# A fixed TensorE order from the last latents to the attention heads of a hybrid decoder layer

## The chip, the cores and the metric

One core of a Trainium2 chip runs the whole kernel. The core has a matrix engine (TensorE, in the rows PE, with its weight loads as PEld), a vector engine (VectorE, DVE), a scalar engine (ScalarE, ACT), a general engine (GpSimd, POOL) and a queue engine (SyncE, SP), which here only issues transfers. Each engine works through a queue of its own in order, and semaphores hold an instruction back until its inputs are there. The metric is the device time of one execution in microseconds; the kernel before takes 1210.38 us (median of 3 runs, 1208.66 to 1212.13).

## The reference, cut to what matters

A decoder layer for 256 tokens and a model width of 2048, all float32. After a norm, one input projection feeds two groups of heads: a recurrent group (RWKV-7, 16 heads of 64) and a latent attention group (8 heads of 128 with a rotary part of 64). Their outputs are concatenated and multiplied by `w_out`; a gated feed-forward block follows.

```python
y = rwkv7_scan(r, decay, k, v, -kk, kk * a)      # state of 64x64 per head, token by token
y = ((y - mu) * lax.rsqrt(var + GN_EPS)).reshape(bsz, s, c) * gn_w + gn_b
bonus = jnp.sum(r * k * r_k, axis=-1, keepdims=True) * v
y_rwkv = (y + bonus.reshape(bsz, s, c)) * g
...
q = (rms_norm(c_q, q_norm_g) @ w_uq)             # c_q, c_kv: latents of width 512
kv = (rms_norm(c_kv, kv_norm_g) @ w_ukv)
sc = (q_nope @ k_nope + q_pe @ k_pe) * scale     # causal, softmax, times v
...
y = jnp.concatenate([y_rwkv, y_mla], axis=-1)
x = x + y @ w_out[l]
```

## The kernel before, in words

**Products.** Every float32 weight piece of 128x1024 is loaded by SyncE (`raw`, L127), rounded by ScalarE to a high part (`hi`, L133) and completed by VectorE with a low part (`lo`, L134). Three buffers of each exist. A product is then three passes, high times high, high times low, low times high (`prod_b`, `prod_c`, `prod_a`, L160 to L197). Their results lie in three PSUM buffers named `mm`; two other PSUM sets, `ch` (three) and `at` (two), hold the small products.

**Input projection.** It runs over 35 tiles of 128 columns: first the decay, gate and key tiles, then `r` (9 to 16), `v` (17 to 24), and last eight tiles of latents (27 to 34), four for the queries and four for keys and values. `latent` (L767) scales a tile (`cr`), adds up its squares, splits it into `cl`, and at the end makes the inverse root `rr` (a chain of tiny GpSimd operations, `rsqrt`) and spreads it over all partitions by two products (`bcast`, `rrB`).

**Recurrence.** The 256 tokens are cut into four chunks of 64. Inside a chunk the token-by-token rule becomes a triangular solve. VectorE inverts 32x32 triangles for all heads in 62 dependent steps (`Tq`, L592 and L594), and GpSimd's queue moves them through DRAM to other partitions: `dT` and `dU` out (L596, L603), `TT` and `T11` back (L609, L605). TensorE joins the halves of each triangle (`pR`, L638, then `pT`, L651). `chunk(c)` (L674) then goes over the two halves `hf` of the head pairs. For each it makes `px` (state and local part), VectorE scales it to `XB`, TensorE multiplies by the triangle (`pu`, in the other half of `px`), VectorE and ScalarE copy it to `UV`, TensorE makes the state's change `pS` and the output `py`, VectorE updates the state `ST`, and ScalarE copies `py` to `yt`. A chunk needs the state of the one before.

**Heads.** `up_b` makes a piece of queries or keys from the latents, a loop at L833 the values. `group_norm(w)` normalises half of the recurrent output on VectorE, multiplies it by a gate (`pgate`, TensorE), and transposes it (`pyT`). `scores(h)` makes the masked scores of a head and its softmax (VectorE maximum, ScalarE exponential, VectorE scaling); `attend(h)` transposes them (`ptp`), copies them by ScalarE (`pT`) and multiplies by the values (`po`). The output product `wout` runs over two halves of its 2048 rows, the recurrent heads first, and the last four heads are traced inside its first half.

**Order.** Apart from a block for SyncE at the start (L328), the order of every engine is written by a planner: it goes through the traced instructions in a simulated run, and whenever an engine is free there it takes the ready instruction that was traced first. So later work, latents or queries, slips between the steps of the recurrence. `manual_schedule(engines=...)` instead keeps the traced order for the engines named inside the block; `issue_after(ins)` queues what it encloses behind `ins`.

Of the kernel before, what the change touches and what calls it, by code (L numbers as in the profile page):

```python
# [17 lines left out]
P = 128  # L18
T = 256
# [35 lines left out]
def hybrid_layer(ctx: ExitStack, tc: tile.TileContext, a: dict, out: bass.AP):  # L55
# [576 lines left out]
    for qh in range(2):  # L632
        pr_ = ch("pR")
        for q in range(16):
            qq = qh * 16 + q
            for h in range(2):
                o0 = h * 64 + 32
                PE.matmul(pr_[o0:o0 + 32, q * 32:(q + 1) * 32], G1[qq // 8][qq % 8 // 4][64:96, h * 4 + qq % 4, 32:64],  # L638
                          T11[h][64:96, qq, :], start=True, stop=True, tile_position=(64, o0))
        for h in range(2):  # L640
            o0 = h * 64 + 32
            V.tensor_tensor(RT[o0:o0 + 32, qh * 16:(qh + 1) * 16, :],
                            pr_[o0:o0 + 32].rearrange("p (q s) -> p q s", q=16),
                            mtok[o0:o0 + 32, qh * 16:(qh + 1) * 16].unsqueeze(2).broadcast_to([32, 16, 32]), ALU.mult)
    for qh in range(2):
        pr_ = ch("pT")
        for h in range(2):
            r0, o0 = h * 64 + 32, h * 64
            for q in range(16):
                qq = qh * 16 + q  # L650
                PE.matmul(pr_[o0:o0 + 32, q * 32:(q + 1) * 32], RT[r0:r0 + 32, qq, :],  # L651
                          TT[r0:r0 + 32, qq, 32:64], start=True, stop=True, tile_position=(r0, o0))
        for h in range(2):
            o0 = h * 64
            V.tensor_copy(TT[o0:o0 + 32, qh * 16:(qh + 1) * 16, 32:64],
                          pr_[o0:o0 + 32].rearrange("p (q s) -> p q s", q=16))
# [17 lines left out]
    def chunk(c):  # L674
        w, r = c // 2, c % 2
        rs_ = HS[r]
        for hf in range(2):
            px = ch("px")
            py = ch("py")

            def pairs(dst, terms):
                for n, term in enumerate(terms):
                    for a_ in range(4):
                        p = hf * 4 + a_
                        for h in range(2):
                            lhsT, rhs = term(p, a_, h)
                            PE.matmul(dst[HS[h], a_ * 64:(a_ + 1) * 64], lhsT, rhs,  # L687
                                      start=n == 0 and a_ == 0, stop=True, skip_group_check=True)
# [4 lines left out]
            def local(s):  # L693
                return lambda p, a_, h: (G1[c][hf][:, h * 4 + a_, s * 64:s * 64 + 64], UV[c][:, p, HS[h]])

            pairs(px, ([state(0)] if c > 0 else []) + [local(0)])
            for h in range(2):
                V.tensor_tensor(XB[hf][HS[h], :, HS[h]], px[HS[h], 0:256].rearrange("p (a v) -> p a v", a=4),
                                mtok[HS[h], c * 8 + hf * 4:c * 8 + hf * 4 + 4].unsqueeze(2).broadcast_to([64, 4, 64]),
                                ALU.mult)  # L700
            pu = px[:, 256:512]
            pairs(pu, [lambda p, a_, h: (TT[:, c * 8 + p, :], XB[hf][:, a_, HS[h]])])
            for h in range(2):
                (S.copy if h else V.tensor_copy)(UV[c][64:128, hf * 4:hf * 4 + 4, HS[h]],
                                                 pu[HS[h]].rearrange("p (a v) -> p a v", a=4))
            if c < 3:
                pS = ch("pS")
                pairs(pS, [lambda p, a_, h: (BKt[c][:, p, HS[h]], UV[c][:, p, HS[h]])])
            pairs(py, ([state(1)] if c > 0 else []) + [local(1)])
            if c < 3:  # L710
                for h in range(2):
                    hs = HS[h]
                    sv = ST[hf][hs, :, hs]
                    pSv = pS[hs, 0:256].rearrange("p (a v) -> p a v", a=4)
                    pcb = PC[hs, hf * 4:hf * 4 + 4, c:c + 1].broadcast_to([64, 4, 64])
                    if c > 0:
                        V.tensor_tensor(sv, pSv, sv, ALU.add)
                        V.tensor_tensor(sv, sv, pcb, ALU.mult)
                    else:
                        V.tensor_tensor(sv, pSv, pcb, ALU.mult)  # L720
            for h in range(2):
                yv = yt[w][rs_, hf * 512:(hf + 1) * 512].rearrange("p (a h v) -> p a h v", a=4, h=2)
                ylast[c] = S.copy(yv[:, :, h, :], py[HS[h], 0:256].rearrange("p (a v) -> p a v", a=4)).ins

    def group_norm(w):
# [19 lines left out]
        V.tensor_tensor(y, y, sq, ALU.add)  # L745
        for j in range(2):
# [4 lines left out]
            V.tensor_tensor(y[:, cs], y[:, cs], pg, ALU.mult)  # L751
        for j in range(2):
# [8 lines left out]
    for c in range(4):  # L761
        chunk(c)


    cl, rrs, rrB = [], [], []

    def latent(x, gname, post):  # L767
        c_ = [s4(F32R, "cl").rearrange("p (k s t) -> p k s t", k=2, s=2) for _ in range(2)]
        ssum = t2("css")
        for j in range(4):  # L770
            acc = in_tile(27 + x * 4 + j)
            cr = t2("cr")
            V.tensor_tensor(cr, acc[:, :T], rsB, ALU.mult)
            if j == 0:
                S.activation(ssum, cr, AF.Square)
            else:
                sq = t2("csq")
                S.activation(sq, cr, AF.Square)
                V.tensor_tensor(ssum, ssum, sq, ALU.add)
            h_, l_ = (c_[j // 2][:, j % 2, q, :] for q in range(2))  # L780
            S.activation(h_, cr, AF.Copy, scale=vv(gname, j))
            V.scalar_tensor_tensor(l_, cr, vv(gname, j), h_.bitcast(F32), ALU.mult, ALU.subtract)
        pss = at("pss")
        for tb in range(2):
            PE.matmul(pss[:, tb * 2:tb * 2 + 2], ssum[:, tb * P:(tb + 1) * P], ones[:, 0:2], start=True, stop=True)
# [4 lines left out]
        rb = con([P, T], f"rrB{x}")  # L790
        bcast(rr, rb, at, t2)
        rrs.append(rr)
        rrB.append(rb)
        cl.append(c_)

    latent(0, "qg", SC)
    latent(1, "kvg", 1.0)
    flush(True)
    qr = s4(n="qr").rearrange("p (h t) -> p h t", h=4)
# [6 lines left out]

    def up_b(src, i, x, dsts):
        pcs = piece(src[i])
        for j in range(2):
# [3 lines left out]
            V.tensor_tensor(dsts[j], acc[:, :T], rrB[x], ALU.mult)  # L813

    for i in range(4, 6):
        up_b(a["wuq"], i, 0, [qr[:, (i - 4) * 2 + j, :] for j in range(2)])
    for j in range(4):
        nc.gpsimd.dma_start(qs[j * 32:(j + 1) * 32], qr[(j ^ 1) * 32:(j ^ 1) * 32 + 32])
    V.tensor_tensor(qr, qr, cosR.unsqueeze(1).broadcast_to([P, 4, T]), ALU.mult)
    V.tensor_tensor(qs, qs, sinR.unsqueeze(1).broadcast_to([P, 4, T]), ALU.mult)  # L820
    V.tensor_tensor(qr, qr, qs, ALU.add)
    g2a = s4(n="g2a")
    g2b = s4(n="g2b")
    gnwb = [s4(n=n) for n in ("gnw", "gnb")]
    with tc.issue_after(ylast[1]):
        for t, n in zip(gnwb, ("gnw", "gnb")):
            nc.scalar.dma_start(t, a[n].broadcast_to([P, 1024]))
        nc.scalar.dma_start(g2a, a["g2"][0:P])
        nc.scalar.dma_start(g2b[64:96], a["g2"][P:160])
# [3 lines left out]
    for cc in range(2):  # L833
        accs = [mm() for _ in range(2)]
        for i in range(2):
            prod_a(accs, piece(a["wuv"][cc, i]), lambda k: cl[1][k // 2][:, k % 2, 0, :],
                   lambda k: cl[1][k // 2][:, k % 2, 1, :],
                   i * 2, 2, i == 0, i == 1)
        for tb in range(2):
# [40 lines left out]
    for i in range(4):  # L880
        up_b(a["wuq"], i, 0, [qn[:, i * 2 + j, :] for j in range(2)])
        up_b(a["wuk"], i, 1, [kn[:, i * 2 + j, :] for j in range(2)])

    def heads(*hs):
        for h in hs:
            scores(h)
            if h > 0:
                attend(h - 1)

    group_norm(0)  # L890
    heads(0, 1)
    group_norm(1)
    heads(2, 3)
# [11 lines left out]
    for half in range(2):  # L905
        if half == 1:
            attend(7)
            zs = [hl4("z") for _ in range(4)]
        for c in range(4):
            accs = [mm() for _ in range(2)]  # L910
            for i in range(4):
                if half == 0 and i == 2:
                    load_x1(c)
                    heads(4 + c)
# [4 lines left out]
            if half == 1:  # L919
# [180 lines left out]
```

## Time and profile before

| | |
|---|---|
| median of 3 runs | 1210.38 us (1208.66 to 1212.13) |
| profiled execution | 1211.12 us, its span 1209.3 us |
| TensorE busy | 1166.8 us, 96% of the span, 7633 products |
| VectorE busy | 819.8 us, 68% |
| ScalarE busy | 583.2 us, 48% |
| GpSimd busy | 82.1 us, 7% |
| mean granted TensorE clock | 0.985 |
| DMA, mean over the span | 179 GB/s |

The span runs from the first to the last instruction. A row of the timeline names start, duration, engine, line, operation, output and inputs and a count; in square brackets stands how long the engine was idle before it and what ended that wait. A wait row has the waiting instruction on the left, its releaser on the right, then the sum, the number and the longest. The granted clock is a share of full speed, and the stretch that the change touches runs from about 221 to 475 us.

### The profile page before, as it was taken

To read this page: it belongs to the slowest core of one execution; us is meant where nothing else is said; L and a number is where in the kernel's file an instruction comes from. 1 tells how busy PE (TensorE), PEld (TensorE's weight loads), DVE (VectorE), ACT (ScalarE), POOL (GpSimd) and SP (SyncE) were. 2 spreads that over 40 slices of the span, in tenths; PEclk is the share of its full clock that TensorE was granted. 3 is DMA by queue.
4 is the path that set the end of the run, shared out by engine and by line. 5 is a ranking of instruction groups with operands and counts; after the bars stand their busy time and mean duration, and the time that the engine had idled before them with its cause. 6 is when DMAs were issued, how large, how long until landed. Compare 5 with 4: busy or idle time off the path is not lost.

```text
span 1209.3 us, 19618 instructions
## 1 busy us (share of the span) xinstructions
PE 1166.8 (96%) x7633; PEld 1029.2 (85%) x7633; DVE 819.8 (68%) x1304; ACT 583.2 (48%) x883; POOL 82.1 (7%) x248
## 2 busy tenths in 40 slices
PE   7899989988798999999999999999999999999996
PEld 7899989987686888888888888888888888888885
DVE  6797659766777556777777776444577777775563
ACT  6674335432334445655555554333455555554442
POOL 1500430301101001000000000000000000000000
PEclk9999999988899999999999999999999999999998
DMA  8555454734142555555555555556655555566672
GB/s 325 164 159 158 147 167 156 209 108 144 54 157 85 170 187 184 183 188 192 190 192 190 191 191 191 191 191 191 205 194 187 192 192 190 192 219 209 209 211 85
DMA packets 61486, 215.90 MB, mean 179 GB/s; under 512 B 7376, under 2 KB 8144, under 8 KB 61392
## 3 DMA queue, kind: packets, MB, share of 16 engines
q1 hardware_dynamic: 58544, 209.22, 52.8%
q0 software_dynamic: 2080, 3.38, 1.3%
q10 hardware_dynamic: 768, 2.05, 0.5%
q8 instruction: 60, 0.98, 0.3%
q14 instruction: 34, 0.28, 0.1%
HBM read 210.48 MB, written 3.41 MB: 177 GB/s over the span
## 4 chain that ended last, share of the span: by engine, by line
PE 87%; DVE 5%; POOL 2%; DMA 2%; ACT 2%; issue 1%; SPq 0%; ACTq 0%; DVEq 0%; POOLq 0%
PE mm L163 27%; PE mm L166 13%; PE mm L195 9%; PE mm L196 9%; PE mm L197 9%; PE mm L175 9%; PE mm L178 4%; PE pg L536 1%; DVE lo L134 1%; DMA T<-dU 1%; ACT hi L133 1%; DMA xraw<-in_xT 1%; PE py L687 1%; PE px L687 1%; POOL sinR L304 0%
## 5 line engine op out<-in xcount | busy, mean ns | idle before, releaser
L134 DVE TENSOR_TENSOR lo<-raw,hi 128x1024 fp32r<-128x1024 f32 x376 | 460.2, 1224 | 287.6 <-ACT hi L133 281.3
L133 ACT CAST hi<-raw 128x1024 fp32r<-128x1024 f32 x376 | 394.9, 1050 | 490.6 <-issue 223.6
L163 PE MATMUL mm<-z,hi 128*128 128x512 f32 x1408 | 351.3, 392 | 0.0
L163 PEld LDWEIGHTS mm<-z,hi 128*128 128x128 f32 x1408 | 251.9, 188 | 43.7
L166 PEld LDWEIGHTS mm<-z,lo 128*128 128x128 f32 x1408 | 188.3, 188 | 14.5
L166 PE MATMUL mm<-z,lo 128*128 128x256 f32 x1408 | 191.6, 278 | 0.0
L175 PE MATMUL mm<-x,hi 128*128 128x256 f32 x1056 | 147.8, 289 | 14.5 <-ACT hi L133 8.1
L175 PEld LDWEIGHTS mm<-x,hi 128*128 128x128 f32 x1056 | 135.4, 195 | 17.1 <-ACT hi L133 8.1
L196 PE MATMUL mm<-lo,hh 128*128 128x512 f32 x336 | 130.7, 389 | 0.0
L197 PE MATMUL mm<-hi,hl 128*128 128x512 f32 x336 | 130.7, 389 | 0.0
L195 PE MATMUL mm<-hi,hh 128*128 128x512 f32 x336 | 119.7, 389 | 0.0
L178 PE MATMUL mm<-x,lo 128*128 128x256 f32 x528 | 77.4, 286 | 0.0
L197 PEld LDWEIGHTS mm<-hi,hl 128*128 128x128 f32 x336 | 63.1, 188 | 13.2
L195 PEld LDWEIGHTS mm<-hi,hh 128*128 128x128 f32 x336 | 63.1, 188 | 13.0
L196 PEld LDWEIGHTS mm<-lo,hh 128*128 128x128 f32 x336 | 63.1, 188 | 13.0
L178 PEld LDWEIGHTS mm<-x,lo 128*128 128x128 f32 x528 | 69.6, 193 | 0.2
L196 PE MATMUL mm<-lo,yhi 128*128 128x512 f32 x128 | 51.5, 403 | 0.0
L197 PE MATMUL mm<-hi,ylo 128*128 128x512 f32 x128 | 50.5, 394 | 0.0
L195 PE MATMUL mm<-hi,yhi 128*128 128x512 f32 x128 | 49.7, 406 | 0.0
L974 POOL MEMSET gt<- 128x2 f32 x44 | 4.3, 99 | 575.9 <-DVE hl L986 559.0
L197 PEld LDWEIGHTS mm<-hi,ylo 128*128 128x128 f32 x128 | 24.2, 189 | 5.1
L196 PEld LDWEIGHTS mm<-lo,yhi 128*128 128x128 f32 x128 | 24.2, 189 | 5.0
(282 smaller groups left out, 1113.1 us busy)
## 6 DMA issues: line engine op xcount, KB each, us to landing
raw<-in_wgu SPq DMA_DIRECT2D x176, 512.0 KB, 3.3
raw<-in_wdn SPq DMA_DIRECT2D x88, 512.0 KB, 4.2
raw<-in_win SPq DMA_DIRECT2D x70, 512.0 KB, 3.6
raw<-in_wout SPq DMA_DIRECT2D x32, 512.0 KB, 3.6
raw<-in_wuq SPq DMA_DIRECT2D x6, 512.0 KB, 4.0
xraw<-in_xT SPq DMA_DIRECT2D x4, 512.0 KB, 6.3
xt<-in_x SPq DMA_DIRECT2D x4, 512.0 KB, 6.8
raw<-in_wuv SPq DMA_DIRECT2D x4, 512.0 KB, 3.8
```

What stands on the lines that cost most here:

```text
L133: S.copy(hi, raw)
L134: last_lo[0] = V.tensor_tensor(lo, raw, hi.bitcast(F32), ALU.subtract).ins
L163: PE.matmul(acc, hi[:, j * P:(j + 1) * P], act(kt0 + j), start=first and j == 0, stop=False, skip_group_check=True)
L166: PE.matmul(acc[:, :T], lo[:, j * P:(j + 1) * P], act(kt0 + j)[:, 0, :], start=False, stop=last and j == n - 1, skip_group_check=True)
L175: PE.matmul(acc, hi[:, j * P:(j + 1) * P], act(kt0 + j)[:, s, :], start=first and j == 0 and s == 0, stop=False, skip_group_check=True)
L178: PE.matmul(acc, lo[:, j * P:(j + 1) * P], act(kt0 + j)[:, 0, :], start=False, stop=last and j == n - 1, skip_group_check=True)
L195: PE.matmul(accs[tb], ah, wh, start=first and j == 0, stop=False)
L196: PE.matmul(accs[tb], ah, wl, start=False, stop=False)
L197: PE.matmul(accs[tb], al, wh, start=False, stop=last and j == n - 1)
L536: PE.matmul(pg[h][:, o:o + P], BK[pp][hs, gg, w * 2 + r, :, :], AR[pp][hs, gg, w * 2 + r, :, :], start=o == 0, stop=True, skip_group_check ...
L687: PE.matmul(dst[HS[h], a_ * 64:(a_ + 1) * 64], lhsT, rhs, start=n == 0 and a_ == 0, stop=True, skip_group_check=True)
L974: nc.gpsimd.memset(gt[:, 0:2], 0.0)
```

## The change

The last latents, the joining of the triangles, the recurrence, the group norms' products, the queries, keys and values and the heads 0 to 5 (with the scores of head 6) are put in one block in which TensorE's order is the traced one. Only the first three tiles of the query latent are traced ahead of it, and stay with the planner.

The loops over `pR` and `pT` become `solve_r` and `solve_t`, unchanged. Each chunk is cut into three steps, and each step runs over both halves: `chunk_a` makes `px`, and for chunks after the first the state's part of `py`; `chunk_b` makes `pu`; `chunk_c` makes `pS` and the local part of `py`. `px` now lies in the `at` buffers, `py` and `pS` in `ch`. Between the steps a generator hands out big products in units: half a latent tile, one piece of queries or keys, or half a piece of values, 24 in all. The group norm is cut into a VectorE part, a gate and an output part.

The query latent's inverse root is no longer spread and multiplied into the queries: ScalarE copies them as they are, and the root goes into the softmax, as the scale of the exponential and a product with the maximum. The halves of the output product change places: the attention rows come first, with the scores of head 7 and the last two `attend` inside its first column block.

```diff
+    def solve_r():
...
+    def solve_t():
...
-    def chunk(c):
+    def chunk_a(c):
         for hf in range(2):
-            px = ch("px")
-            py = ch("py")
+            px[hf] = at("px")
+            if c > 0:
+                py[hf] = ch("py")
+                pairs(py[hf], hf, [state(1)])
+            pairs(px[hf], hf, ([state(0)] if c > 0 else []) + [
+                lambda p, a_, h: (G1[c][hf][:, h * 4 + a_, 0:64], UV[c][:, p, HS[h]])])
...
+    def chunk_b(c):
+        for hf in range(2):
+            pu = px[hf][:, 256:512]
+            pairs(pu, hf, [lambda p, a_, h: (TT[:, c * 8 + p, :], XB[hf][:, a_, HS[h]])])
...
+    def chunk_c(c):
+        for hf in range(2):
             if c < 3:
                 pS = ch("pS")
+                pairs(pS, hf, [lambda p, a_, h: (BKt[c][:, p, HS[h]], UV[c][:, p, HS[h]])])
...
+        for hf in range(2):
+            if c == 0:
+                py[hf] = ch("py")
+            pairs(py[hf], hf, [...], c == 0)
...
+    def latent_tile(x, j, gname):
...
+        prod_c(acc, piece(a["win"][i, 0]), x_hl, 0, 8, True, False)
+        yield
+        prod_c(acc, piece(a["win"][i, 1]), x_hl, 8, 8, False, True)
...
-            V.tensor_tensor(dsts[j], acc[:, :T], rrB[x], ALU.mult)
+            if x == 0:
+                S.copy(dsts[j], acc[:, :T])
+            else:
+                V.tensor_tensor(dsts[j], acc[:, :T], rrB1, ALU.mult)
...
             V.tensor_reduce(mx[:, qb:qb + 1], psc[:, ks], AX.X, ALU.max, negate=True)
-            S.activation(pe_[:, ks], psc[:, ks], AF.Exp, bias=mx[:, qb:qb + 1], accum_out=sm[:, qb:qb + 1])
+        V.tensor_tensor(mx, mx, rrs[0], ALU.mult)
+        for qb in range(2):
+            ks = slice(qb * P, qb * P + (qb + 1) * P)
+            S.activation(pe_[:, ks], psc[:, ks], AF.Exp, bias=mx[:, qb:qb + 1], scale=rrs[0][:, qb:qb + 1],
+                         accum_out=sm[:, qb:qb + 1])
...
+    for j in range(3):
+        for _ in latent_tile(0, j, "qg"):
+            pass
...
+    def all_units():
+        yield from latent_tile(0, 3, "qg")
+        for j in range(4):
+            yield from latent_tile(1, j, "kvg")
+            if j == 0:
+                latent_rs(0, SC)
+        up_b(a["wuq"], 4, 0, [qr[:, j, :] for j in range(2)])
+        yield
+        latent_rs(1, 1.0)
+        up_b(a["wuq"], 5, 0, [qr[:, 2 + j, :] for j in range(2)])
+        rope_q()
+        yield
...
+        bcast(rrs[1], rrB1, mm, t2)
+        up_b(a["wuk"], 0, 1, [kn[:, j, :] for j in range(2)])
+        yield
+        yield from up_v(0)
...
+    with tc.manual_schedule(engines={mybir.EngineType.PE}):
+        solve_r()
+        unit(2)
+        solve_t()
+        chunk_a(0)
+        unit(2)
+        chunk_b(0)
+        unit()
+        chunk_c(0)
+        for c in range(1, 4):
+            unit()
+            chunk_a(c)
+            unit()
+            chunk_b(c)
+            unit()
+            chunk_c(c)
...
+        gn_vec(0)
+        gn_vec(1)
+        unit(2)
+        scores(0)
+        unit()
+        scores(1)
+        attend(0)
+        gn_gate(0)
+        unit()
+        gn_out(0)
+        attend(1)
+        scores(2)
+        unit()
+        scores(3)
+        attend(2)
+        unit()
+        attend(3)
+        unit(2)
+        gn_gate(1)
+        scores(4)
+        unit()
+        scores(5)
+        attend(4)
+        gn_out(1)
+        unit()
+        attend(5)
+        scores(6)
...
-    for half in range(2):
-        if half == 1:
-            attend(7)
+    for half in (1, 0):
+        if half == 0:
             zs = [hl4("z") for _ in range(4)]
...
-                if half == 0 and i == 2:
+                if half == 1 and i == 2:
                     load_x1(c)
-                    heads(4 + c)
+                if half == 1 and c == 0 and i in (1, 2, 3):
+                    (scores(7), attend(6)) if i == 1 else attend(7) if i == 3 else None
```

More of the change, by code (lines that the diff above doesn't have):

```diff
@@ L631, in hybrid_layer @@
     RT = sv("RT").rearrange("p (q s) -> p q s", q=32)
[L632 to L635, printed above, removed]
+    def solve_r():
+        for qh in range(2):
+            pr_ = ch("pR")
+            for q in range(16):
+                qq = qh * 16 + q
+                for h in range(2):
+                    o0 = h * 64 + 32
+                    PE.matmul(pr_[o0:o0 + 32, q * 32:(q + 1) * 32], G1[qq // 8][qq % 8 // 4][64:96, h * 4 + qq % 4, 32:64],
+                              T11[h][64:96, qq, :], start=True, stop=True, tile_position=(64, o0))
@@ L645, in hybrid_layer @@
[L645 to L656, printed above, removed]
+                V.tensor_tensor(RT[o0:o0 + 32, qh * 16:(qh + 1) * 16, :],
+                                pr_[o0:o0 + 32].rearrange("p (q s) -> p q s", q=16),
+                                mtok[o0:o0 + 32, qh * 16:(qh + 1) * 16].unsqueeze(2).broadcast_to([32, 16, 32]), ALU.mult)
@@ L670, in hybrid_layer, with pairs @@
     ylast = [None] * 4
-    def chunk(c):
-        w, r = c // 2, c % 2
-        rs_ = HS[r]
-        for hf in range(2):
-            px = ch("px")
-            py = ch("py")
[L681 to L688, printed above, removed]
+    def pairs(dst, hf, terms, first=True):
+        for n, term in enumerate(terms):
+            for a_ in range(4):
+                p = hf * 4 + a_
+                for h in range(2):
+                    lhsT, rhs = term(p, a_, h)
+                    PE.matmul(dst[HS[h], a_ * 64:(a_ + 1) * 64], lhsT, rhs,
+                              start=first and n == 0 and a_ == 0, stop=True, skip_group_check=True)
@@ new lines, in hybrid_layer, with unit @@
+    units = all_units()
+    def unit(n=1):
+        for _ in range(n):
+            next(units)
+    with tc.manual_schedule(engines={mybir.EngineType.PE}):
[14 more added lines that the diff above has]
+            chunk_c(c)
+        g2a = s4(n="g2a")
+        g2b = s4(n="g2b")
+        gnwb = [s4(n=n) for n in ("gnw", "gnb")]
+        with tc.issue_after(ylast[1]):
+            for t, n in zip(gnwb, ("gnw", "gnb")):
+                nc.scalar.dma_start(t, a[n].broadcast_to([P, 1024]))
+            nc.scalar.dma_start(g2a, a["g2"][0:P])
+            nc.scalar.dma_start(g2b[64:96], a["g2"][P:160])
+        gn_vec(0)
[25 more added lines that the diff above has]
+        scores(6)
+        assert next(units, None) is None
```

138 lines of the change are left out of this document (63 added, 75 removed).

## The prediction

> **What bounds the kernel now.** I read the page first (the engines' shares: TensorE is busy 96% of a span of 1209.3 us, nothing else over 68%), then the table of stretches, then the waits of TensorE inside the stretch that the change touches, from the last latents to the end of the output product. In the table of stretches the columns are length, busy time with count for PE, PEld, DVE, ACT, POOL, then the granted clock, DMA share and GB/s.
>
> ```profile
> PE 1166.8 (96%) x7633; PEld 1029.2 (85%) x7633; DVE 819.8 (68%) x1304; ACT 583.2 (48%) x883; POOL 82.1 (7%) x248
> ```
>
> ```profile
> 221.00:475.00 254.00, 235.71 (x2053) 202.55 (x2052) 167.97 (x268) 101.13 (x173) 26.50 (x69) 0.95 0.45 141
> 254.00:261.00 7.00, 7.00 (x62) 6.82 (x59) 3.74 (x6) 1.04 (x1) 0.00 (x0) 0.51 0.16 64
> 295.00:301.00 6.00, 5.05 (x89) 4.87 (x91) 3.54 (x8) 1.10 (x3) 0.00 (x0) 0.50 0.48 157
> 322.00:330.00 8.00, 6.92 (x68) 6.32 (x67) 5.09 (x9) 3.94 (x8) 0.00 (x0) 0.57 0.57 192
> 373.00:377.00 4.00, 3.13 (x13) 3.06 (x14) 2.67 (x6) 1.68 (x4) 0.00 (x0) 0.57 0.00 0
> ```
>
> The first row holds everything that can be won: 254.0 - 235.7 = 18.3 us in which TensorE does nothing. The other four rows are the places where it works at about half the clock; busy time times the missing share of the clock is 7.00 x 0.49 + 5.05 x 0.50 + 6.92 x 0.43 + 3.13 x 0.43 = 3.4 + 2.5 + 3.0 + 1.3 = 10.2 us. Together 28.5 us are lost in this stage, and a perfect order of TensorE could win no more.
>
> The waits of TensorE in the same stretch (us in all, times, longest) say where the 18.3 us lie:
>
> ```profile
> PE px L687 <- DVE XB L698: 5.5, 5, 2.7
> PE pyT L755 <- DVE yt L751: 4.1, 1, 4.1
> PE mm L178 <- DVE lo L134: 2.0, 1, 2.0
> PE pS L687 <- DVE UV L704: 2.0, 3, 0.8
> PE py L687 <- DVE ST L717: 1.9, 1, 1.9
> PE pR L638 <- DMA T<-dU: 1.4, 1, 1.4
> ```
>
> The recurrence (the px, pS and py rows) and the group norm (pyT) cost most; the wait for the solved triangles (pR, for T) costs only 1.4 us. Why only 1.4 is what this prediction turns on, so the timeline of TensorE around it comes next (start, duration, instruction, count):
>
> ```profile
> 221.45 2.04 PE L175 MATMUL mm<-x,hi 128*128 128x256 f32 x16
> ...
> 224.28 2.05 PE L175 MATMUL mm<-x,hi 128*128 128x256 f32 x16
> ...
> 241.69 0.63 PE L175 MATMUL mm<-x,hi 128*128 128x256 f32 x4
> 243.77 0.28 PE L638 MATMUL pR<-T,G 32*32 32x32 f32 x4 [1.45 <-DMA T<-dU]
> ...
> 246.41 2.21 PE L638 MATMUL pR<-T,G 32*32 32x32 f32 x124
> 248.54 0.71 PE L237 MATMUL rsb<-dg,ones 128*128 128x128 f32 x4
> ...
> 250.78 4.30 PE L651 MATMUL pT<-TT,RT 32*32 32x32 f32 x128
> ```
>
> Up to 241.69 TensorE multiplies latents (L175): half a latent tile every 224.28 - 221.45 = 2.83 us. They are the filler under which the triangles go through DRAM. Where the third latent tile ends follows from VectorE, which reads each finished tile once (L773), and the chain of T from VectorE's last step and GpSimd's queue:
>
> ```profile
> 221.65 0.42 DVE L773 TENSOR_TENSOR cr<-mm,rsB 128x256 f32<-128x256 f32 x1 [0.35 <-PE mm L178]
> ...
> 224.62 1.22 DVE L134 TENSOR_TENSOR lo<-raw,hi 128x1024 fp32r<-128x1024 f32 x1
> 225.76 0.21 DVE L594 TENSOR_TENSOR Tq<-Tq,tm 128x31 f32<-128x31 f32 x1
> ```
>
> ```profile
> 226.28 1.00 POOL L596 DMA_DIRECT2D dT<-Tq  x1 [36.62 <-DVE Tq L594]
> 227.44 1.00 POOL L603 DMA_DIRECT2D dU<-tp  x2 [0.17 <-issue]
> 232.14 3.16 POOL L609 DMA_DIRECT2D TT<-dT  x4 [3.69 <-DMA dT<-Tq]
> 235.29 0.79 POOL L605 DMA_DIRECT2D T<-dU  x1
> ...
> 236.39 0.81 POOL L605 DMA_DIRECT2D T<-dU  x1
> ```
>
> ```profile
> qs<-qr POOLq DMA_DIRECT2D x4, 128.0 KB, 3.6
> ...
> T<-dU POOLq DMA_DIRECT2D x2, 128.0 KB, 8.4
> ```
>
> The third finished latent tile is read at 221.65 (the earlier ones 5.66 us apart); the triangles are done at 225.97, go out, come back, and the second T lands at 236.39 + 8.4 = 244.8.
>
> **The change part by part.**
>
> *Wait for T.* The new order puts only the first three latent tiles ahead of the fixed block, and the block begins with the pR products. Everything that TensorE did from 221.45 to 241.69 now stands behind pR in its queue: the fourth tile of the first latent, the second latent, and through them all units, steps, heads. So TensorE arrives at 221.45 and stands. What VectorE does up to that point is the same program, so Tq ends hardly earlier: one split (the lo at 224.62) falls away, because three pieces are then already held and TensorE frees none; 1.2 us. T is then issued last at about 235.2. How long it takes to land is unknown, since hardly any weights are then loading beside it: between 3.6 us (qs, the same size, but not through DRAM) and 8.4 us (now). It lands between 238.8 and 243.6; I take the middle, 241.2. The wait is 20 us (17.4 to 22.2).
> The Trainium skill, in "DMA: Bandwidth & Descriptors", section Specifications, gives 512 bytes as the least run for full rate. T is stored to DRAM and reread in runs of 32 floats, 128 bytes, and by that rule the missing weights would help it little and the wait would be the 22 us of the upper end; the trace has the 8.4 us, but none without weights beside it.
>
> *What is removed.* At best the whole 28.5 us: all waits, T's 1.4 among them, and all half clock. Row by row: px waits for XB, pS for UV and py for ST get a unit of 2.83 us between the steps, which is longer than the longest of them (2.7). The 4.1 us for yt go because the gate of the second half now stands eight units later. The rrB broadcast of the first latent (L237) goes, at most 0.7 us; I take 0.5. Its 12 multiplications move from VectorE to a ScalarE copy and the softmax gets one tiny product more per head; I cost both at nothing: three mm buffers and a unit of 2.83 us cover the copy, and without that cover each of the 12 would cost its 0.42 us (the L773 row, same shape), 5 us in all, which the high end of the units below includes.
>
> *New half clock.* After 20 us of standing TensorE starts pR at half clock. The nearest rows are the 4.1 us wait (373 to 377: 1.3 us lost) and the run of small products (254 to 261: 3.4 us lost; there it had been busy with pT from 250.78 on and the clock still fell). I take 3.4 for the start, and half of another 3.4 for pT, which again runs 4.3 us of 32x32 products alone: 5 us (1.3 to 8).
> The Trainium skill's page "TensorE: Matmul & The Clock Gate", Part 1, has the clock halve after an idle window of some 3.4 us and return after as long a busy one; by that the start would cost 1.7 us. The 7 us at half clock from 254 agree with the drop but not with so quick a return.
>
> *New waits in the recurrence.* A step now belongs to both halves, and three `ch` buffers hold py, py and one pS. So the second pS must wait until VectorE has read the first.
>
> ```profile
> 281.04 0.87 DVE L717 TENSOR_TENSOR ST<-pS,ST 64x256 f32<-64x256 f32 x2
> ```
>
> That is 0.9 us plus some 0.3 of signals, or up to 1.2 more when a split or a step of the group norm (the lo row and the yt row below) is under way: 1.2 to 2.4 for chunks 1 and 2, less for chunk 0 (py waits there): 3 to 7.
>
> ```profile
> 371.78 1.22 DVE L745 TENSOR_TENSOR yt<-yt,gsq 128x1024 f32<-128x1024 f32 x1
> ```
>
> ```profile
> L133 ACT CAST hi<-raw 128x1024 fp32r<-128x1024 f32 x376 | 394.9, 1050 | 490.6 <-issue 223.6
> ```
>
> VectorE's own work per chunk (14 operations of about 0.42, as the two of the L717 row, and three splits of 1.22, near 11 us with a latent tile's) fills most of the 12 us of a chunk, so XB and ST slip past their 2.83 us now and then: 0 to 4. I take 6 us together (3 to 11).
>
> *New waits in the heads.* In `attend` the three transposes are followed at once by po, which needs ScalarE's copy. Now:
>
> ```profile
> 360.76 0.38 PE L872 MATMUL ptp<-cst,pexp 128*128 128x128 f32 x2
> ...
> 361.18 0.48 ACT L873 COPY pT<-ptp 128x384 f32<-128x384 f32 x1 [1.65 <-PE ptp L872]
> ...
> 361.84 0.59 PE L875 MATMUL po<-pT,vm 128*128 128x256 f32 x2
> ```
>
> From the transposes' end (361.14) to po it takes 0.7 us, filled at present with another head's scores. Six `attend` lie in the fixed block: 0.7 each, or 1.75 behind one of ScalarE's casts of 1.05 (the L133 row); 4.2 to 10.5, I take 6. The softmax has one unit and one score ahead of its transposes (about 4.3 us), and the two group norms, traced before the heads, put VectorE operations of 1.22 us ahead of their maxima and of the splits: 0 to 7, I take 3. The output product now begins with the attention half, whose last two heads are just being made: 0 to 3, I take 1. New waits: 6 + 6 + 3 + 1 = 16 (7 to 31; not all will be at their worst, so I carry 25).
>
> *Sum.* New losses 20 + 5 + 16 = 41 (25.7 to 55) against 28.5 + 0.5 removed: +12 us (-3 to +26). The profiled execution took 1211.1 us, its span and 1.8 us around it, and lies 0.7 above the median of the runs. 1211.1 + 12 = 1223.1, against the median 1222.4: I say 1222.
>
> **The rivals.**
>
> 1. *The steps are covered (faster).* Place: the gaps between the steps of each chunk and after each ptp. Each old wait was at most 2.7 us and each unit is 2.83, which speaks for it. If units cover all but the floor of the `attend` copies (4.2), T lands as fast as qs (17.4), and the clock recovers in 1.3, new losses are 22.9 against 29: -6, 1204 us. It decides from the point where all new waits after T stay under 29 - 20 - 5 = 4 us with my T; the six copies alone use 4.2, which speaks against it. Chance 0.14.
>
> 2. *It evens out.* The idle time is only moved: one long wait in place of many. With T at its fast end (17.4), 3 us of half clock and 8 of new waits, 28.4 against 29: 1210 us. For it: VectorE does the same work in the stage (168 of 254 us). Against it: the wait for T has no cover at all now. Chance 0.14.
>
> 3. *VectorE becomes the bound of the heads (slower still).* Both group norms (some eight operations of 1.22 us each, near 20 us) come up when the last chunk ends, ahead of splits and maxima; TensorE's fixed order can no longer slip other work in. With T at 22, half clock 7 and new waits 25 the sum is 54 - 29 = +25: 1235 us. Against it: in the stretch VectorE is busy only 168 of 254 us. Chance 0.14.
>
> 4. *The wait for T doesn't come.* The block's first products might still be passed by later latents, if the order did not bind TensorE. Then the recurrence alone is rearranged: 29 - 16 - 5 = 8 us won, 1202 us. Nothing in the trace speaks for it: the pR products now already make TensorE stand while L175 work is at hand. Chance 0.03; it goes with the faster cases.
>
> **How the numbers follow.** The forecast (slower, +4 to +20 us, 1214 to 1230) has 0.55. Anything within 0.3% (3.6 us) counts as no change here, as the runs before spread that far. Slower: 0.55 + 0.14 + a part of the second case that ends above +3.6 = 0.71. Faster: 0.14 + 0.03 less what stays within 3.6 us = 0.14. Same: 0.15. The range takes in the first rival's price at its low end and the third's at its high end: 1204 to 1235.
>
> **What would show it.** Right: the longest wait of TensorE is pR for T, 17 to 22 us, beginning near 221.5 with pR's start near 241; the px and ST waits of the recurrence fall under 1 us each; pS waits for ST in chunks 1 and 2 (1 to 2.5 us); po waits for pT six times, about 1 us each; the clock is near 0.5 for some us behind pR. Wrong: a wait for T under 12 us, or sums of waits behind T under 4 us, would turn the sign; a group norm row (yt or gva) at the head of TensorE's or VectorE's waits would mean the third rival.

## The result, and the profile after

The changed kernel takes 1241.66 us (median; 1235.73 to 1243.22) against 1209.52 us for the kernel before on the same chip: a ratio of 1.0246, 95% interval 1.0225 to 1.0267. It is slower, as forecast, but by some 32 us, not 12, and it lies above the range.

The page of the changed kernel, shares of the engines and the slices of the span (40 equal ones of 31 us):

```profile
PE 1173.2 (95%) x7629; PEld 1031.4 (83%) x7629; DVE 815.6 (66%) x1297; ACT 588.7 (47%) x895; POOL 82.8 (7%) x248
...
PE   7899989599759999999999999999999999999996
...
PEclk9999999689959999999999999999999999999998
```

The span grew from 1209.3 to 1240.8 us, by 31.5. TensorE is busy 6.4 us more for four products fewer, which fits the lower clock (17.1 us lost to it against 10.2, worked out below); the other 25 us are idle time. TensorE's share sags in slice 8 and in slices 11 and 12, its clock in slices 8 and 9 and in slice 12. The waits of TensorE in the changed kernel (us in all, times, longest) name them:

```profile
PE ptp L899 <- DVE pexp L891: 17.0, 1, 17.0
PE pR L640 <- DMA T<-dU: 15.1, 2, 14.6
...
PE po L902 <- ACT pT L900: 4.4, 5, 1.8
...
PE pS L685 <- DVE ST L728: 3.0, 2, 1.9
PE py L685 <- DVE UV L713: 1.8, 2, 1.2
PE py L685 <- DVE ST L731: 0.8, 1, 0.8
```

The first two waits make 17.0 + 15.1 = 32.1 us. The rows of before that were to go (px for XB 5.5, pyT for yt 4.1, mm for lo 2.0) are gone. The table of stretches of the changed kernel, same columns as before:

```profile
236.00:246.00 10.00, 9.37 (x160) 9.20 (x161) 3.36 (x5) 1.05 (x1) 0.00 (x0) 0.58 0.01 3
250.00:259.00 9.00, 9.00 (x127) 8.82 (x123) 4.88 (x10) 0.89 (x1) 0.00 (x0) 0.62 0.19 60
284.00:290.00 6.00, 4.95 (x64) 4.87 (x65) 4.13 (x11) 1.46 (x4) 0.00 (x0) 0.72 0.25 87
322.00:328.00 6.00, 5.95 (x30) 4.75 (x31) 5.95 (x8) 3.17 (x6) 1.72 (x2) 0.72 0.54 175
336.00:353.00 17.00, 0.13 (x1) 0.13 (x1) 13.46 (x21) 3.14 (x9) 5.10 (x14) 0.62 0.17 62
353.00:367.00 14.00, 13.43 (x30) 6.75 (x31) 5.05 (x9) 0.85 (x2) 0.00 (x0) 0.50 0.00 0
```

Busy time times the missing share of the clock gives 3.9 us behind the first long wait, 3.4 behind the transposed triangles, 1.4 and 1.7 in the recurrence, and 6.7 behind the second long wait: 17.1 us, where the kernel before lost 10.2.

What TensorE waits for from 336 to 353 is in VectorE's timeline of the changed kernel (start, duration, instruction):

```profile
328.62 1.22 DVE L744 TENSOR_REDUCE gmu<-yt 128x16 f32<-128x1024 f32 x1
...
333.29 1.23 DVE L752 TENSOR_TENSOR yt<-yt,ry 128x1024 f32<-128x1024 f32 x1 [2.20 <-POOL ry L228]
...
340.22 1.22 DVE L760 TENSOR_TENSOR yt<-yt,gsq 128x1024 f32<-128x1024 f32 x1
342.62 1.22 DVE L750 TENSOR_REDUCE gva<-gsq 128x16 f32<-128x1024 f32 x1 [1.18 <-ACT gsq L748]
343.88 2.45 DVE L757 TENSOR_TENSOR gsq<-UV,bon 64x1024 f32<-64x1024 f32 x2
346.34 0.62 DVE L882 TENSOR_REDUCE mx<-psc 128x1 f32<-128x128 f32 x2
```

TensorE's side of the same stretch:

```profile
329.84 0.34 PE L871 MATMUL psc<-cmb,idb 128*128 128x384 bf16 x1
...
335.24 0.59 PE L878 MATMUL psc<-kpe,qr 128*128 128x256 f32 x2
...
352.87 0.95 PE L899 MATMUL ptp<-cst,pexp 128*128 128x128 f32 x3 [17.04 <-DVE pexp L891]
```

The scores of head 0 begin at 329.84, and the block gives TensorE one unit and the scores of head 1 after them, up to 335.8. The maximum of head 0 comes only at 346.34, since VectorE first goes through both group norms: the first ends at 340.22 + 1.22 us, and the larger part of the second (gmu at 328.62, gva and gsq from 342.62 on) also stands ahead. That VectorE stood still for 2.20 and 1.18 us in between, waiting for GpSimd's root and ScalarE's squares, shows that this is a chain and not only a load. The scores of head 0 were finished at 331.5, so for 1.8 of the 2.20 us and all of the 1.18 us their maximum could have been made; VectorE's own order, which is the planner's, held it behind the norms.

### The profile page after: what moved, and what is told of

Same layout as the page of the kernel before. It is cut to its first block, busy times and chain, and to the rows that moved or that the text cites. A ratio compares the mean times of both kernels' runs of the same rounds, so it can differ in the third digit from the quotient of the medians.

```text
span 1240.8 us, 19622 instructions
## 1 busy us (share of the span) xinstructions
PE 1173.2 (95%) x7629; PEld 1031.4 (83%) x7629; DVE 815.6 (66%) x1297; ACT 588.7 (47%) x895; POOL 82.8 (7%) x248
## 4 chain that ended last, share of the span: by engine, by line
PE 89%; DVE 3%; DMA 3%; POOL 2%; ACT 1%; issue 1%; ACTq 0%; SPq 0%; DVEq 0%
PE mm L163 26%; PE mm L166 13%; PE mm L175 11%; PE mm L195 9%; PE mm L196 9%; PE mm L197 9%; PE mm L178 5%; DMA raw<-in_win 2%; DVE lo L134 1%; PE pg L536 1%; ACT hi L133 1%; PE px L685 1%; PE pgate L768 0%; PE pgate L767 0%; PE po L902 0%
## 5 line engine op out<-in xcount | busy, mean ns | idle before, releaser
L175 PEld LDWEIGHTS mm<-x,hi 128*128 128x128 f32 x1056 | 137.1, 197 | 17.9 <-ACT hi L133 8.4
L195 PEld LDWEIGHTS mm<-hi,yhi 128*128 128x128 f32 x128 | 24.0, 188 | 7.2 <-DVE x L1015 1.0
```

The lines of the kernel that those rows point to most:

```text
L175: PE.matmul(acc, hi[:, j * P:(j + 1) * P], act(kt0 + j)[:, s, :], start=first and j == 0 and s == 0, stop=False, skip_group_check=True)
L195: PE.matmul(accs[tb], ah, wh, start=first and j == 0, stop=False)
```

## The experiments

The theory after the result: the two long waits come from where the fixed order puts things (triangles with nothing ahead of them, group norms ahead of the softmax). The rival: fixing TensorE's order costs wherever the pieces stand, because each removed wait reappears elsewhere. All ratios are against the kernel before in the same comparison (its median there 1210.72, 1211.48 or 1210.83). They are the ratios on record and not quotients of these medians: in the first comparison (both norms behind the scores, units ahead, heads planned, everything planned) the kernel before lay between 1208.91 and 1220.54, and ratio and quotient differ by up to 0.4%. Differences of 4 us between variants are therefore not read as gains by themselves.

**Both group norms behind the scores.**

```diff
-        gn_vec(0)
-        gn_vec(1)
         unit(2)
         scores(0)
         unit()
         scores(1)
+        gn_vec(0)
...
         scores(3)
+        gn_vec(1)
         attend(2)
```

> The changed kernel with the vector part of the first group norm traced behind the scores of head 1 and that of the second behind the scores of head 3; TensorE's order is the same. Theory A (VectorE's order: the softmax of head 0 queues behind both group norms): the 17.0 us wait of ptp for pexp falls under 4 us, the half clock after it (7.0 us) goes, about 1220 us (1215 to 1226). Rival B (VectorE has no room in the heads, whatever its order): the wait turns up at yt, pyT or lo instead, 1233 us or more.

1234.38 us, ratio 1.0162 (1.0114 to 1.0209). Waits of TensorE in this variant:

```profile
PE pR L640 <- DMA T<-dU: 14.9, 2, 14.6
PE pyT L776 <- DVE yt L769: 13.2, 1, 13.2
...
PE ptp L899 <- DVE pexp L891: 1.1, 1, 1.1
```

VectorE's timeline of this variant:

```profile
332.99 1.21 DVE L744 TENSOR_REDUCE gmu<-yt 128x16 f32<-128x1024 f32 x1
...
347.70 1.23 DVE L752 TENSOR_TENSOR yt<-yt,ry 128x1024 f32<-128x1024 f32 x1 [3.26 <-POOL ry L228]
...
352.74 1.29 DVE L769 TENSOR_TENSOR yt<-yt,pgate 128x512 f32<-128x512 f32 x2
```

The wait of 17.0 falls to 1.1, so the group norms had made it. But 13.2 us come up where the norm's result is transposed: from gmu to the gated yt the norm takes 354.0 - 333.0 = 21 us, and the order holds too little in that time. Of the 24 us (wait and clock) only 7.3 came back by the medians. In its outcome the rival is right here; its reason, that VectorE has no room in whatever order, is not borne out: VectorE was idle for 3.26 us inside this very chain, and the order laid out anew, further down, has no such wait.

**Only the second norm behind the scores.**

```diff
         gn_vec(0)
-        gn_vec(1)
...
         scores(3)
+        gn_vec(1)
         attend(2)
```

> Only the second head's group norm (its vector part) is moved behind the fourth scores; the first one stays where it was. Theory (the wait for pexp is the time that VectorE spends on two norms ahead of the first maximum): one norm is left ahead, the wait of 17.0 falls to about 6 and no long wait arises at the output products, since the first norm's chain of some 20 us still starts early: about 1225. Rival (the first norm alone holds VectorE as long, because its chain waits for GpSimd in between): the wait stays over 12, the time over 1235.

1230.59 us, ratio 1.0154 (1.0136 to 1.0171). Waits of TensorE in this variant:

```profile
PE ptp L899 <- DVE pexp L891: 8.4, 2, 7.3
```

With one norm ahead the longest wait is 7.3, and pyT no longer waits. The direction is that of the theory; the time is 5.6 us above its figure and the wait nearer to it than to the rival's 12.

**Units ahead of the triangles.** The five units of the solver and of chunk 0 go in front of the first pR.

```diff
     with tc.manual_schedule(engines={mybir.EngineType.PE}):
+        unit(5)
         solve_r()
-        unit(2)
         solve_t()
         chunk_a(0)
-        unit(2)
         chunk_b(0)
-        unit()
         chunk_c(0)
```

> The changed kernel with the first five units ahead of the pR products, and none in the solve and chunk 0. Theory A (TensorE stands because nothing is traced ahead of pR): the wait for T falls from 15.1 us to under 2, the half clock at 236 to 246 (3.9 us) goes, and solve and chunk 0 pay 6 to 9 us for RT, TT, XB and UV without cover: about 1231 us (1226 to 1235). Rival B (T itself comes later when TensorE and the weights run beside it, as in the kernel before): T lands near 244 and the wait stays over 6 us, 1238 us or more.

1233.75 us, ratio 1.0153 (1.0112 to 1.0193). Waits of TensorE in this variant:

```profile
PE pR L640 <- DMA T<-dU: 8.5, 2, 7.7
```

Five units are some 14 us of products (5 x 2.83), and the wait fell only by 6.6, because T came later. The DMA issues (last figure: median us from issue to landing), first of the changed kernel, then of this variant:

```profile
dT<-Tq POOLq DMA_DIRECT2D x1, 512.0 KB, 3.3
TT<-dT POOLq DMA_DIRECT2D x4, 128.0 KB, 3.7
...
T<-dU POOLq DMA_DIRECT2D x2, 128.0 KB, 4.3
```

```profile
dT<-Tq POOLq DMA_DIRECT2D x1, 512.0 KB, 5.5
TT<-dT POOLq DMA_DIRECT2D x4, 128.0 KB, 6.0
...
T<-dU POOLq DMA_DIRECT2D x2, 128.0 KB, 8.7
```

While weights are loading, every hop of the triangles through DRAM takes longer. It is the loading that goes with it, not TensorE's work: in this variant T, issued at 234.8 and 235.5, took 8.7 us although TensorE stood still from 235.7 to 243.4, and the two weight pieces issued at 234.1 and 237.2 took 8.6 and 8.2 us themselves. In the changed kernel SyncE issued no piece between 223.3 and 246.6.

So the rival has the mechanism right (T lands near 244, the wait stays over 6 us), but not its time of 1238 or more. The time falls into theory A's range by luck: the half clock that A let go stayed (some 6.4 us lost between 242 and 261), and the 6 to 9 us that it charged for missing cover hardly came (XB 0.4 us).

**The solver's second step parted.** One unit goes between the two halves of the pT products.

```diff
         solve_r()
-        unit(2)
-        solve_t()
+        unit()
+        solve_t((0,))
+        unit()
+        solve_t((1,))
```

> The changed kernel with the run of 32x32 and small products after T is back parted into two by a unit of weights. Theory (a run of small products on end lets the granted clock fall, which costs 3.4 us between 250 and 259 us): the clock in that stretch stays near 1 and the time falls by 3 to 4, to about 1238. Rival (the clock falls there for the wait for T just ahead, whatever follows): the clock falls as far, the time stays at 1241 to 1242.

1236.63 us, ratio 1.0223 (1.0196 to 1.0251). That interval overlaps with the changed kernel's, so the time alone decides nothing; the stretches of this variant do:

```profile
250.00:259.00 9.00, 9.00 (x148) 8.76 (x150) 6.58 (x12) 2.98 (x5) 0.00 (x0) 1.00 0.22 68
```

The clock stays at 1.00 where it had been 0.62, with the same wait for T (15.1) ahead, so the rival is refuted and one unit in the middle of the small products is enough to keep the clock up here. A rise between 284 and 290 (0.72 to 1.00) came with it and was not expected. That every such run lets the clock fall is not shown: in the order laid out anew with the old halves (below), the 128 pT products also run on end, from 252.55 on for 3.93 us, and the stretch around and behind them reads

```profile
252.50:264.00 11.50, 10.61 (x257) 10.04 (x257) 8.68 (x14) 2.01 (x4) 0.00 (x0) 1.00 0.29 93
```

There the clock had been low just before (0.50 from 248 to 250). What tells the two cases apart stays open.

**The heads left to the planner.** The block ends behind chunk_c(3); the same code after it is traced in the same order, but TensorE's order in it is the planner's.

```diff
             unit()
             chunk_c(c)
-        gn_vec(0)
-        gn_vec(1)
...
+    gn_vec(0)
+    gn_vec(1)
...
```

> The changed kernel with the fixed block ended behind the last chunk; the heads are left to the planner, and the traced order is the same. Theory A (the fixed order cannot fill the softmax's wait): units fill it, the 17.0 us and 7.0 us of half clock and most of the 4.4 us for pT go: about 1215 us (1210 to 1222). Rival B (VectorE is the bound of the heads): 1233 us or more.

1219.51 us, ratio 1.0051 (1.0028 to 1.0074): 22 us less than the changed kernel, and inside theory A's range. Waits of TensorE in this variant:

```profile
PE pR L640 <- DMA T<-dU: 14.8, 2, 14.5
...
PE ptp L899 <- DVE pexp L891: 2.4, 1, 2.4
```

**Everything left to the planner.** Same tracing, no block at all.

```diff
-    with tc.manual_schedule(engines={mybir.EngineType.PE}):
+    if True:
         solve_r()
```

> The changed kernel with no fixed order at all: steps, units and heads are traced in the same order, TensorE follows the planner. Theory A (the fixed order itself makes the two long waits): both go, 1205 to 1215 us. Rival C (the rewritten steps and the exchanged halves cost, whatever the order): 1225 us or more.

1204.15 us, ratio 0.9914 (0.9879 to 0.9948): faster than both kernels, though against the kernel before by less than 1%. So the fixed order, as it was placed, costs 1241.66 - 1204.15 = 37.5 us, and the rest of the change (steps over both halves, buffers, scaling, exchanged halves) is worth some 7 us by the medians and 10 by the ratio; which part of it brings that is not shown. The wait for T is 1.9 us. Two groups of rows show what became of the softmax. TensorE in this variant:

```profile
314.04 0.34 PE L871 MATMUL psc<-cmb,idb 128*128 128x384 bf16 x1
...
347.90 0.27 PE L899 MATMUL ptp<-cst,pexp 128*128 128x128 f32 x1
```

VectorE in this variant:

```profile
328.18 1.21 DVE L750 TENSOR_REDUCE gva<-gsq 128x16 f32<-128x1024 f32 x1
329.43 2.45 DVE L757 TENSOR_TENSOR gsq<-UV,bon 64x1024 f32<-64x1024 f32 x2
331.89 0.62 DVE L882 TENSOR_REDUCE mx<-psc 128x1 f32<-128x128 f32 x2
```

From the first scores to the first maximum it takes 331.89 - 314.04 = 17.9 us, more than the 346.34 - 329.84 = 16.5 in the changed kernel, and the norms stand ahead of it all the same. VectorE is no quicker. The planner has merely put other products in front of the transposes: of the 347.90 - 314.04 = 33.9 us from the first scores to them TensorE waits for 3.6 and works for the rest. In the changed kernel they come 352.87 - 329.84 = 23.0 us after the first scores, and the fixed order holds work for 6.

**The fixed order laid out anew.** Eight units ahead of the triangles, one between the steps of the solver, one in chunk 0; `attend` cut into transposes and products with a unit or another head's scores between; norms and gates spread.

```diff
+        unit(8)
         solve_r()
-        unit(2)
+        unit()
         solve_t()
...
         gn_vec(0)
-        gn_vec(1)
-        unit(2)
+        unit()
         scores(0)
         unit()
         scores(1)
-        attend(0)
-        gn_gate(0)
+        attend_t(0)
         unit()
-        gn_out(0)
-        attend(1)
+        attend_o(0)
         scores(2)
+        attend_t(1)
+        unit()
+        attend_o(1)
+        gn_gate(0)
+        scores(3)
+        gn_vec(1)
...
```

> The order stays fixed by hand, but is laid out anew: a unit of weights goes ahead of the solver's last reads, one stands between the steps of chunk 0, the attend steps are parted into the transposes and the products with a unit between, and the group norms of the two earlier heads come behind the scores that they had stood ahead of, each cut into its vector part and its gate. Theory (both long waits come from where the work was placed, not from the order being fixed): the 17 us wait for pexp and its 7 us at half clock go, the wait for T falls to about 8 as it did with a unit ahead, 1241.7 - 24 - 7 = about 1210. Rival (a fixed order can't follow what VectorE and the transfers do, wherever the pieces stand): another wait of over 8 us arises in the heads, and the time stays over 1225.

1206.7 us, ratio 0.996 (0.9944 to 0.9976): 0.4% under the kernel before, and 35 us faster than the changed one. Waits of TensorE in this variant:

```profile
PE rsb L237 <- DVE dg L236: 4.7, 1, 4.7
...
PE px L685 <- DVE XB L703: 3.2, 1, 3.2
...
PE pR L640 <- DMA T<-dU: 1.0, 1, 1.0
```

Neither long wait is left, and none over 8 us arises in the heads. With eight units ahead of it, not one, the wait for T is 1.0 us instead of the 8 that were expected. So most of what the fixed order cost lay in its placing. Against everything left to the planner (1204.15) this order is 2.6 us behind, and the two intervals just overlap.

**The exchange of the output product's halves.** It was undone in the planned variant and in the order laid out anew.

```diff
-    for half in (1, 0):
+    for half in range(2):
```

> The variant with everything left to the planner (1204.15), with the output product's halves in their old order, so that the exchange of halves alone is undone. Theory (the gain of that variant comes from the recurrence's three steps and its own buffers, the exchange of halves is worth at most the 3 us that the prediction gave it): 1204 to 1207. Rival (the exchange is where the 6 us came from): 1209 to 1211.

> The fixed order as laid out anew, with the output product's halves in their old order. Theory (the exchange of the halves gives nothing, since nothing waits there in either order): within 3 us of the 1206.7 of the order laid out anew. Rival (the old order of the halves is better by what the two planned variants lay apart, 1204.15 against 1197.85): about 1200.

Planned: 1197.85 us, ratio 0.989 (0.9864 to 0.9916), an interval that overlaps with that of the exchanged order. It lies under both expectations, which had the old halves equal or slower. Laid out anew: 1206.59 us, ratio 0.9964 (0.9952 to 0.9976), equal to 1206.7, as the theory said. So the exchange gives nothing that can be seen with the fixed order; whether it costs some us with the planner stays open. The planned variant with the old halves is the fastest kernel of all; it lies 8.7 us under the order laid out anew with the same halves, and their intervals do not overlap. So the best order by hand that was tried still costs something against the planner (`attend` is cut in the one and whole in the other).

**The steps traced on end.** In that fastest variant, the three steps of a chunk and then its units; the five units of the solver and of chunk 0 come behind chunk 0 in the same way.

```diff
         for c in range(1, 4):
-            unit()
             chunk_a(c)
-            unit()
             chunk_b(c)
-            unit()
             chunk_c(c)
+            unit(3)
```

> The planned variant with the old halves, where each chunk's three steps are traced on end and the units behind them, so that the planner alone can put units between the steps. Theory (what the planner does with the pieces, not the order in which they are traced, gives the gain over before): within 3 us of 1197.85. Rival (the traced order of step, unit, step is what hides the waits inside a chunk): the waits for XB and for the state come back, 5 to 10 us, 1203 to 1208.

1200.24 us, ratio 0.9923 (0.9906 to 0.994), 2.4 from the interleaved tracing. Waits of TensorE in this variant:

```profile
PE psc L871 <- ACT pexp L886: 7.2, 2, 6.9
...
PE px L685 <- DVE XB L703: 0.2, 1, 0.2
```

The wait for XB is 0.2 (1.2 with the units traced between the steps), and no wait for the state comes back. The wait of 6.9 us that comes up is in the heads (scores behind the exponentials of an earlier head), and the wait for T is 4.0. So the rival's waits don't arise: the planner puts units between the steps by itself, in whichever order they are traced.

## Why the prediction was wrong in its size

**The term that failed: "the two group norms ... put VectorE operations of 1.22 us ahead of their maxima and of the splits: 0 to 7, I take 3".** It was 17.0 us of waiting and, behind it, 6.7 us at half clock. The mechanism was seen (it is also the third rival, at 0.14), but it was sized by a few operations in the way. The chain of waiting and working from the scores to the maximum is 16.5 us, with GpSimd and ScalarE in it, and the softmax follows; 23.0 us in all until the transposes, and all of it but the 6 us of work that the order holds becomes a wait. That such chains are long could be read in the kernel before, in VectorE's rows of the second norm:

```profile
355.17 1.21 DVE L729 TENSOR_REDUCE gmu<-yt 128x16 f32<-128x1024 f32 x1
...
373.04 1.28 DVE L751 TENSOR_TENSOR yt<-yt,pgate 128x512 f32<-128x512 f32 x2
```

From gmu to the gated yt it takes 374.3 - 355.2 = 19 us there, of which only the last 4.1 showed as a wait (pyT for yt). In that kernel the second norm also stood behind the first scores, whose maximum began at 353.76, 1.9 us after the first of their products of queries and keys. The argument brought against the rival, that VectorE is busy only 168 of 254 us, says nothing: VectorE was idle for parts of the very wait that its order caused (13.46 of 17 us busy).

**The wait for T: 20 (17.4 to 22.2) predicted, 15.1 measured.** Arrival at 221.5 and the mechanism were right, and dT went out 1.2 us earlier, as foreseen. The step that failed here is that only the last hop was allowed to get faster; the reload was to go out last at "about 235.2", and went out at 232.6. GpSimd's timeline of the changed kernel:

```profile
225.06 0.89 POOL L596 DMA_DIRECT2D dT<-Tq  x1 [35.16 <-DVE Tq L594]
226.12 1.00 POOL L603 DMA_DIRECT2D dU<-tp  x2 [0.17 <-issue]
228.63 3.16 POOL L609 DMA_DIRECT2D TT<-dT  x4 [1.51 <-DMA dT<-Tq]
231.78 1.56 POOL L605 DMA_DIRECT2D T<-dU  x2
```

dT landed in 3.3 instead of 5.6 us, and with its earlier start TT and the first T were issued 3.5 us earlier than before; T then took 4.3, near the low end of 3.6 to 8.4. The sentence on the Trainium skill's 512-byte rule ("DMA: Bandwidth & Descriptors", Specifications) goes the wrong way with it: that rule would have left the reload slow, at a wait of 22 us, and these 128-byte runs took 8.4 beside weight loads and 4.3 without them.

**Half clock: 5 (1.3 to 8) for the start and pT; 3.9 + 3.4 = 7.3 measured,** in the range. The 3.4 for pT is the row of before, repeated. What was not counted is 6.7 us behind the second long wait and 3.1 us in the recurrence; the former belongs to the failed term. By the rule of the Trainium skill's page "TensorE: Matmul & The Clock Gate", Part 1, the start would cost 1.7 us; the 3.9 disagree with it. Nor does the stretch from 254 in the kernel before meet that rule's condition for the drop, though the prediction calls them in agreement: TensorE was busy there without a break (7.00 of 7 us, and pT for 4.30 ahead of it), so no idle window of that length stood in front.

**The recurrence: 6 (3 to 11) predicted, 5.6 measured** (pS 3.0, py 1.8 and 0.8); the two waits of pS for ST are 1.91 and 1.07 us, against 1.2 to 2.4 each. **The copies in `attend`: 6 (4.2 to 10.5), 4.4 measured,** in five waits, not six. **What was removed** went as the sum had it: the rows for XB, yt and lo are gone, and pS no longer waits for UV.

**The sum again,** with measured terms: 15.1 (T) + 17.1 (half clock) + 5.6 (recurrence) + 4.4 (attend) + 17.0 (softmax) = 59.2 against 29 removed: +30.2, where the span grew by 31.5. The sum was made of the right parts, and one of them was nearly six times too small. Taking the half clock behind that wait with it, the failed term is 23.7 - 3 = 20.7 us short, and the wait for T gave 5 back.

**The rivals.** Covered steps (1204): the steps were covered as it said, but it left out the softmax. Evening out (1210): refuted by the 59 us. VectorE the bound (1235): right in its place, 24 us at the softmax's transposes alone, and nearest to the result, though the row that was to show it (yt or gva at the head of the waits) is not there: the head is ptp for pexp. It is not a bound of VectorE's capacity, though: with the same work on VectorE, the planned variant takes 1204.15. No wait for T (1202): refuted by 15.1 us.

Of the 28.5 us of which the prediction said that "a perfect order of TensorE could win no more", the fastest variant won 1211.48 - 1197.85 = 13.6.

## What to carry to other kernels

When an engine's order is fixed by hand, price each dependent product by the whole chain of the other engines that leads to it (here 16.5 us from scores to maximum, 21 for a group norm), not by the operations that seem to be in the way, and count how many microseconds of independent work the order holds in that time (here 6). A planner that hides a chain leaves little or no wait in the profile before (4.1 of a norm's 19 us here), so the chain's length must be read from start to start on the two engines; their shares of busy time don't show it. Before fixing an order, try the same pieces with the order left free: here that was worth more than the order (1204.15 against 1241.66, and 1206.7 for the order by hand laid out anew).

## What the runs showed of the hardware

The DMA issues of the kernel before, to stand beside those of the changed kernel and of the variant with units ahead:

```profile
dT<-Tq POOLq DMA_DIRECT2D x1, 512.0 KB, 5.6
TT<-dT POOLq DMA_DIRECT2D x4, 128.0 KB, 5.9
```

The transfers of the triangles through DRAM (the reloads T and TT in runs of 128 bytes, the store dT in whole rows of a tile) took a half to two thirds as long while no weights were loading, or for dT hardly any: T 4.3 us against 8.4 before and 8.7 with units ahead, TT 3.7 against 5.9 and 6.0, dT 3.3 against 5.6 and 5.5. That TensorE stood still too made no difference to T with units ahead: it took 8.7 us with TensorE idle for most of them. So in this kernel a wait in which no weights are loading shortens itself, and work that is put ahead of it wins less than its length: five units took 6.6 us off the wait.

The granted clock of the changed kernel fell to 0.62 in a stretch where TensorE is shown busy all the time (9.00 of 9 us). It fell at 251.2, some 3 us into 4.4 us of 32x32 products on end, and stayed at 1.00 when one unit of 128-row products stood between their halves. Another order ran the same products on end at 1.00, so such a run does not always have this effect; how long it may be wasn't tried.
